# Weighted combine of expert outputs on one core: who copies the weights of a round, and how the first tail tokens are loaded

## The chip, the cores and the metric

The kernel runs on one NeuronCore of one Trainium2 chip. The metric is the device time of one execution in microseconds; the number compared is the median over several executions. One execution is also profiled, and the profile's times are counted from the start of its span.

## The reference

For each of 16 x 1024 = 16384 tokens there are 8 expert outputs of 512 numbers and 8 weights. The result is the weighted sum over the experts.

```python
batch, seq, n_experts, expert_dim = 16, 1024, 8, 512
weights = combine_weights[..., np.newaxis]
return np.sum(expert_outputs * weights, axis=2).astype(np.float32)
```

All is float32. The input is 268.4 MB, the output 33.6 MB.

## The kernel before, in words

**Tiles.** Every partition owns 121 tokens that are worked in a loop of 11 rounds (`ROUNDS`) of 11 tokens (`R`), and 7 tail tokens (`TAIL`). `ring` holds one round's input, 11 tokens of 8 x 512 numbers in each partition. A round is cut into three chunks, of 4, 4 and 3 tokens (`CHUNKS`, line 41); a chunk of 4 tokens is 8.39 MB over the 128 partitions, and a round with its store is 25.95 MB. There is one ring, so a chunk of the next round can be loaded only when the same chunk of this round has been worked. `sums` holds one round's results, also once.

**SyncE** (`loads_and_last_stores`, lines 126 to 145) issues all input loads in order, on one DMA queue: per round three chunk loads, then the tail tokens, then the last round's store, then the two stores of the tail. Before each chunk load it waits for two semaphores:

```python
sync.wait_ge(copied, (n - 1) * C + c + 1)
sync.wait_ge(w_set, n * C + c + 1)
```

**GpSimd** (`weights_and_store`, lines 160 to 171) copies a chunk's weights of the coming round from `w_t`, where all weights lie, to `w_c`, where the loop of VectorE reads them at a fixed address; it does so when `copied` says that the chunk of this round is worked and copied out. `w_set` counts these copies. At one place, after the first copy for the last round, it also runs `store_apart` (lines 106 to 117): a part of the store of round 9, in three DMAs of its own, and a fourth small DMA (`turn`, line 119). These are counted on `rest_out`, and ScalarE waits for them before the first copy of round 10 (line 190).

**VectorE** (`terms`, lines 229 to 295) does the sums: per chunk one product over the chunk (line 250), then for experts 1 to 7 one multiply-and-add for each token (line 242), in place in `ring`. In chunks of 4 tokens two tokens take turns, in the chunk of 3 all three. The last multiply-and-add of each token counts `done` up by 1 (line 235).

**ScalarE** (`copies_stores_and_diagonals`, lines 173 to 203) waits for a chunk's `done`, copies the results to `sums` (line 175), counts `copied`, and after the third chunk issues the round's store on its own DMA queue (line 185). It begins the copies of a round only when the store of the round before has landed (`stored`, line 179), as there is one `sums`.

**The tail.** The 7 tail tokens go to the ring places of chunks 0 and 1: one load for tokens 0 to 2, then four loads of one token (`tail_loads`, line 65). TensorE forms the first 3 to 5 terms of each tail token with diagonal matrices that ScalarE makes (lines 205 to 227); VectorE adds the rest (lines 269 to 295). TensorE starts when the first tail load has landed (line 217).

Of the kernel before, what the change touches and what calls it, by code (L numbers as in the profile page):

```python
# [10 lines left out]
def kernel(  # L11
# [21 lines left out]
    nc = tc.nc  # L33
# [6 lines left out]
    R = 11  # L40
    CHUNKS = [(0, 4), (4, 4), (8, 3)]
    C = len(CHUNKS)
    T_P = T // P
    ROUNDS = T_P // R
    LOOP = ROUNDS * R
    TAIL = T_P - LOOP
# [3 lines left out]
    SHARED = ROUNDS - 2  # L50
# [8 lines left out]
    x_t = x[cut:T].rearrange("(p j) e d -> p j e d", j=TAIL)  # L59
# [2 lines left out]


    pe_e = [4, 4, 3, 4, 4, 5, 4]
    tail_loads = [(0, 3)] + [(j, 1) for j in range(3, TAIL)]
    tail_stores = [(0, 5), (5, 2)]
    loads = [k for k, (j, m) in enumerate(tail_loads) for _ in range(m)]
    diags = [(j, e) for j in range(TAIL) for e in range(pe_e[j])]

    one = ctx.enter_context(tc.tile_pool(name="one", bufs=1))  # L70
# [1 line left out]
    ring = one.tile([P, R, E, D], fp32, name="ring")  # L72
    sums = one.tile([P, R, D], fp32, name="sums")
    w_t = one.tile([P, T_P, E], fp32, name="w_t")
    w_c = one.tile([P, R, E], fp32, name="w_c")
# [3 lines left out]
    diag = one.tile([P, DIAGS, P], fp32, name="diag")  # L79
    ps = psum.tile([P, TAIL, D], fp32, name="ps")  # L80

    last_sums = ring[:, TAIL + 1, 1 : 1 + TAIL]

    sem = tc.alloc_semaphore
    w_in = sem("w_in")
    w_set = sem("w_set")
    loaded = [sem(f"loaded{c}") for c in range(C)]
    copied = sem("copied")
    here = sem("here")
    stored = sem("stored")  # L90
    rest_out = sem("rest_out")
    step = sem("step")
    done = sem("done")
    tail_in = [sem(f"tail_in{k}") for k in range(len(tail_loads))]
    tail_out = nc.alloc_semaphore("tail_out")
    id_set = sem("id_set")
    diag_set = sem("diag_set")
# [6 lines left out]
        queue.dma_start(out=o_r[n, :, first:], in_=flat[:, first:]).then_inc(stored, 16)  # L104

    def store_apart(gpsimd):
        flat = sums.rearrange("p g d -> p (g d)")
        gpsimd.wait_ge(copied, SHARED * C + 1)
        gpsimd.dma_start(  # L109
            out=o_r[SHARED, 0:OURS, 0 : APART * D], in_=flat[0:OURS, 0 : APART * D]  # L110
        ).then_inc(rest_out, 16)
        for k in range(2):
            part = slice(k * APART * D // 2, (k + 1) * APART * D // 2)
            gpsimd.dma_start(out=o_r[SHARED, OURS:P, part], in_=flat[OURS:P, part]).then_inc(  # L114
                rest_out, 16
            )
        turn(gpsimd, 13, 4)

    def turn(gpsimd, k, b):

        gpsimd.dma_start(  # L121
            out=spare[0:k, b : b + 4].rearrange("p (i j) -> p i j", i=2)[:, :, 0:1],
            in_=w[0 : 2 * k].rearrange("(p i) e -> p i e", i=2)[:, :, 0:1],
        ).then_inc(rest_out, 16)

    def loads_and_last_stores(sync):
        for n in range(ROUNDS):
            for c, (r, m) in enumerate(CHUNKS):
                if n:
                    sync.wait_ge(copied, (n - 1) * C + c + 1)  # L130
                    sync.wait_ge(w_set, n * C + c + 1)
                part = slice(r, r + m)
                sync.dma_start(out=ring[:, part], in_=x_r[n, :, part]).then_inc(loaded[c], 16)
                if n == 0 and c == 0:
                    sync.dma_start(out=w_t[:, 0:LOOP], in_=w_r).then_inc(w_in, 16)
                    sync.dma_start(out=w_t[:, LOOP:T_P], in_=w_x).then_inc(w_in, 16)
        for k, (j, m) in enumerate(tail_loads):
            sync.wait_ge(copied, (ROUNDS - 1) * C + (j + m - 1) // 4 + 1)
            sync.dma_start(out=ring[:, j : j + m], in_=x_t[:, j : j + m]).then_inc(tail_in[k], 16)
        store(sync, ROUNDS - 1)  # L140
        for j, m in tail_stores:
            sync.wait_ge(done, LOOP - SHARED * R + j + m)
            sync.dma_start(out=o_t[:, j : j + m], in_=last_sums[:, j : j + m]).then_inc(
                tail_out, 16
            )

    def identity(gpsimd):
# [8 lines left out]
            pattern=[[-1, P]],  # L156
            channel_multiplier=1,
        ).wait_op(id_set, 2, "sem-ge").then_inc(id_set, 1)

    def weights_and_store(gpsimd):  # L160
        turn(gpsimd, 4, 0)
        gpsimd.wait_ge(w_in, 32).then_inc(stored, 16)
        for n in range(ROUNDS):
            for c, (r, m) in enumerate(CHUNKS):
                if n:
                    gpsimd.wait_ge(copied, (n - 1) * C + c + 1)
                gpsimd.tensor_copy(  # L167
                    out=w_c[:, r : r + m], in_=w_t[:, n * R + r : n * R + r + m]
                ).then_inc(w_set, 1)
                if n == SHARED + 1 and c == 0:  # L170
                    store_apart(gpsimd)

    def copies_stores_and_diagonals(scalar):
        def copy(r, m):
# [38 lines left out]

    def first_terms(tensor):
        for k, (j, e) in enumerate(diags):
            if k == 0:
                tensor.wait_ge(tail_in[0], 16)
            if e == 0:
                tensor.wait_ge(tail_in[loads[max(j, 2)]], 16)
            tensor.wait_ge(diag_set, k + 1)  # L220
            tensor.matmul(  # L221
                ps[:, j],
                lhsT=diag[:, k % DIAGS],
                rhs=ring[:, j, e],
                start=e == 0,
                stop=e == pe_e[j] - 1,
            ).then_inc(product, 1)

    def terms(vector):
        last = {}  # L230

        def count(i, g, e):

            if e == E - 1:
                i.then_inc(done, 1)
            else:
                i.then_inc(step, 1)
                last["all"] = last.get("all", 0) + 1
                last[g] = last["all"]

        def fused(total, g, e, weight, before):
            return vector.scalar_tensor_tensor(  # L242
                out=total, in0=ring[:, g, e], scalar=weight, in1=before, op0=mult, op1=add
            )

        vector.wait_ge(w_set, C)
        with nc.Fori(0, ROUNDS, engines=OrderedEngineSet([vector.engine])):  # L247
            for c, (r, m) in enumerate(CHUNKS):
                take(vector, loaded[c], 16)
                i = vector.tensor_tensor(  # L250
                    out=ring[:, r : r + m, 0],
                    in0=ring[:, r : r + m, 0],
                    in1=w_c[:, r : r + m, 0:1].to_broadcast([P, m, D]),
                    op=mult,
                )
                i.then_inc(step, 1)
                last["all"] = last.get("all", 0) + 1
                last.update((g, last["all"]) for g in range(r, r + m))
                for some in [(r, r + 1), (r + 2, r + 3)] if m == 4 else [range(r, r + m)]:
                    for e in range(1, E):  # L260
                        for k in some:
                            i = fused(ring[:, k, 0], k, e, w_c[:, k, e : e + 1], ring[:, k, 0])
                            i.wait_op(step, last[k], "sem-ge")
                            count(i, k, e)
            take(vector, step, last["all"])

        last.clear()

        def tail_term(j, e, end):
            total, x, weight = last_sums[:, j], ring[:, j, e], w_t[:, LOOP + j, e : e + 1]  # L270
            if e > pe_e[j]:
                i = fused(total, j, e, weight, total)
                i.wait_op(step, last[j], "sem-ge")
            elif j < TAIL - 1:
                i = fused(total, j, e, weight, ps[:, j])
                i.wait_op(product, sum(pe_e[: j + 1]), "sem-ge")
            else:
                i = vector.tensor_scalar_mul(out=total, in0=x, scalar1=weight)  # L278
                i.wait_op(tail_in[-1], 16, "sem-ge")
            count(i, j, end)  # L280

        j = TAIL - 1
        for k in range(j - 1):
            for e in range(pe_e[k], E):
                tail_term(k, e, e)

        vector.wait_ge(copied, ROUNDS * C)
        for e in range(pe_e[j], E):
            tail_term(j, e, -1)
            if e + 1 < E:  # L290
                tail_term(j - 1, e + 1, e + 1)
        vector.wait_ge(step, last[j])  # L292
        i = vector.tensor_tensor(out=last_sums[:, j], in0=last_sums[:, j], in1=ps[:, j], op=add)  # L293
        i.wait_op(product, len(diags), "sem-ge")
        count(i, j, E - 1)

    with tc.tile_critical(no_gpsimd_drain=True):  # L297
        loads_and_last_stores(nc.sync)
        identity(nc.gpsimd)
        weights_and_store(nc.gpsimd)  # L300
        copies_stores_and_diagonals(nc.scalar)
        first_terms(nc.tensor)
        terms(nc.vector)
# [35 lines left out]
```

## Time and profile before

| what | value |
|---|---|
| median of 3 runs | 757.14 us (756.41 to 757.99) |
| the profiled execution: its time, its span | 756.85 us, 755.2 us |
| busy share of the span: VectorE, GpSimd, ScalarE, TensorE | 86%, 10%, 9%, 4% |
| moved by DMA, mean rate | 302.54 MB, 401 GB/s |
| busy share of the DMA engines by queue: SyncE's, ScalarE's, GpSimd's | 85.2%, 8.7%, 0.2% |
| granted TensorE clock, mean | 0.999 |

The time of an execution is 1.65 us more than its span. The DMA share of a stretch is the mean over 16 DMA engines of the time that their packets took; a packet is put down whole where it is recorded, so over a few us the share can pass 1, and it is read over longer stretches. The busy time of an engine does not count its waits. Idle time of an engine is put down to what released it.

### The profile page before, as it was taken

The numbers are of one execution on the slowest core, as the hardware profiler recorded it, in microseconds if no ns is written. First come the engines' busy times: TensorE is split into PE (matmuls) and PEld (weight loads), VectorE is DVE, ScalarE is ACT, GpSimd is POOL, SyncE is SP. The second block draws the span as 40 slices with busy tenths as digits, with TensorE's granted clock in tenths as the row PEclk, the third lists the DMA queues.
The fourth block names the chain that finished last, engine by engine and source line by source line (L and its number), as shares of the span: only waits on it lengthen the run. The fifth ranks groups of instructions, "written<-read, shape, count | busy, mean of one in ns | idle before, by whom it ended". The sixth has DMA issues, their size and how long they took to land. (4 is left out here: it accounts for less than half of the span.)

```text
span 755.2 us, 1471 instructions
## 1 busy us (share of the span) xinstructions
PE 27.3 (4%) x56; PEld 11.6 (2%) x56; DVE 652.2 (86%) x909; ACT 68.8 (9%) x63; POOL 74.6 (10%) x45
## 2 busy tenths in 40 slices
PE   0000000000000000000000000000000000000067
PEld 0000000000000000000000000000000000000023
DVE  0699999497999949799994899999479999948998
ACT  0011002001101100110110001011010101101132
POOL 0000006000000600000140000033000005300000
PEclk9999999999999999999999999999999999999999
DMA  9999994999999699999959999996999997899998
GB/s 389 423 437 445 415 427 200 413 403 448 444 439 408 250 382 437 444 444 427 430 240 391 429 444 444 410 410 278 410 432 422 444 434 330 350 385 432 456 408 373
DMA packets 7907, 302.54 MB, mean 401 GB/s; under 512 B 1112, under 2 KB 1112, under 8 KB 1504
## 3 DMA queue, kind: packets, MB, share of 16 engines
q1 hardware_dynamic: 6192, 273.68, 85.2%
q10 hardware_dynamic: 1440, 28.31, 8.7%
q0 software_dynamic: 272, 0.52, 0.2%
q14 instruction: 3, 0.02, 0.0%
HBM read 268.96 MB, written 33.55 MB: 401 GB/s over the span
## 5 line engine op out<-in xcount | busy, mean ns | idle before, releaser
L242 DVE SCALAR_TENSOR_TENSOR ring<-ring,w_c 128x512 f32<-128x512 f32 x847 | 564.1, 745 | 1.2
L250 DVE TENSOR_TENSOR ring<-ring,w_c 128x2048 f32<-128x2048 f32 (+1 forms) x33 | 69.6, 2108 | 98.1 <-DVEq L212 98.1
L167 POOL COPY w_c<-w_t 128x32 f32<-128x32 f32 (+1 forms) x33 | 71.0, 2154 | 585.3 <-ACTq L183 522.0
L175 ACT COPY sums<-ring 128x2048 f32<-128x2048 f32 (+1 forms) x33 | 57.9, 1756 | 669.9 <-ACTq L212 580.6
L221 PE MATMUL ps<-ring,diag 128*128 128x512 f32 x56 | 27.3, 652 | 723.4 <-DMA ring<-in_expert_outputs_dram 723.4
L221 PEld LDWEIGHTS ps<-ring,diag 128*128 128x128 f32 x56 | 11.6, 210 | 738.2 <-DMA ring<-in_expert_outputs_dram 723.4
L242 DVE SCALAR_TENSOR_TENSOR ring<-ring,w_t 128x512 f32<-128x512 f32 x21 | 15.4, 750 | 0.6
L207 ACT ACTIVATE diag<-ident,w_t 128x128 f32<-128x128 f32 x28 | 9.6, 393 | 4.6 <-PE ps L221 4.6
L242 DVE SCALAR_TENSOR_TENSOR ring<-ring,w_t,ps 128x512 f32<-128x512 f32 x6 | 4.5, 742 | 0.0
L121 POOL DMA_DIRECT2D spare<-in_combine_weights_dram x2 | 1.4, 694 | 0.3 <-issue 0.3
L177 ACT ACT_TABLE_LOAD x1 | 1.3, 1283 | 0.9 <-SPq L297 0.9
L114 POOL DMA_DIRECT2D out_dram<-sums x2 | 1.0, 518 | 0.0
L293 DVE TENSOR_TENSOR ring<-ring,ps 128x512 f32<-128x512 f32 x1 | 0.7, 687 | 0.1
L109 POOL DMA_DIRECT2D out_dram<-sums x1 | 0.6, 572 | 0.0
L278 DVE TENSOR_SCALAR ring<-ring,w_t 128x512 f32<-128x512 f32 x1 | 0.5, 480 | 0.0
L150 POOL TENSOR_SCALAR_AFFINE_SELECT ident<-ident 128x128 f32<-128x128 f32 x1 | 0.3, 287 | 0.1
L149 POOL MEMSET ident<- 128x128 f32 x1 | 0.2, 204 | 0.0
L177 ACT COPY warm<-warm 128x1 f32<-128x1 f32 x1 | 0.2, 191 | 0.0
L148 POOL MEMSET warm<- 128x2 f32 x1 | 0.1, 99 | 0.5 <-SPq L297 0.5
L323 POOL MEMSET const-float32-0.0<- 128x1 f32 x1 | 0.1, 100 | 0.2 <-issue 0.2
L323 POOL MEMSET const-uint8-127<- 128x1 uint8 x1 | 0.1, 103 | 0.0
L323 POOL MEMSET const-bfloat16-1.0<- 128x1 bf16 x1 | 0.1, 102 | 0.0
(1 smaller groups left out, 0.1 us busy)
## 6 DMA issues: line engine op xcount, KB each, us to landing
ring<-in_expert_outputs_dram SPq DMA_DIRECT2D x12, 6144.0 KB, 41.4
out_dram<-sums ACTq DMA_DIRECT2D x9, 2816.0 KB, 28.1
ring<-in_expert_outputs_dram SPq DMA_DIRECT2D x4, 2048.0 KB, 22.5
out_dram<-sums SPq DMA_DIRECT2D x1, 2816.0 KB, 17.0
out_dram<-sums ACTq DMA_DIRECT2D x1, 2304.0 KB, 30.3
out_dram<-ring SPq DMA_DIRECT2D x1, 1280.0 KB, 5.6
out_dram<-ring SPq DMA_DIRECT2D x1, 512.0 KB, 3.0
w_t<-in_combine_weights_dram SPq DMA_DIRECT2D x1, 484.0 KB, 22.5
```

Source lines behind the costliest of these rows:

```text
L109: gpsimd.dma_start(out=o_r[SHARED, 0:OURS, 0 : APART * D], in_=flat[0:OURS, 0 : APART * D]).then_inc(rest_out, 16)
L114: gpsimd.dma_start(out=o_r[SHARED, OURS:P, part], in_=flat[OURS:P, part]).then_inc(rest_out, 16)
L121: gpsimd.dma_start(out=spare[0:k, b : b + 4].rearrange("p (i j) -> p i j", i=2)[:, :, 0:1], in_=w[0 : 2 * k].rearrange("(p i) e -> p i e", ...
L167: gpsimd.tensor_copy(out=w_c[:, r : r + m], in_=w_t[:, n * R + r : n * R + r + m]).then_inc(w_set, 1)
L175: return scalar.copy(out=sums[:, r : r + m], in_=ring[:, r : r + m, 0])
L177: scalar.copy(out=warm[:, 1:2], in_=warm[:, 0:1]).wait_op(id_set, 1, "sem-ge")
L207: return scalar.mul(out=diag[:, k % DIAGS], in_=ident, mul=w_t[:, LOOP + j, e : e + 1]).then_inc(diag_set, 1)
L221: tensor.matmul(ps[:, j], lhsT=diag[:, k % DIAGS], rhs=ring[:, j, e], start=e == 0, stop=e == pe_e[j] - 1,).then_inc(product, 1)
L242: return vector.scalar_tensor_tensor(out=total, in0=ring[:, g, e], scalar=weight, in1=before, op0=mult, op1=add)
L250: i = vector.tensor_tensor(out=ring[:, r : r + m, 0], in0=ring[:, r : r + m, 0], in1=w_c[:, r : r + m, 0:1].to_broadcast([P, m, D]), op=mult,)
L278: i = vector.tensor_scalar_mul(out=total, in0=x, scalar1=weight)
L293: i = vector.tensor_tensor(out=last_sums[:, j], in0=last_sums[:, j], in1=ps[:, j], op=add)
```

## The change

VectorE waits once for all weights to have landed. At the head of each round of its loop it copies the round's 11 x 8 weights to `w_c` itself, and the first product of each chunk waits for `step` 1, which that copy counts. GpSimd copies no weights; of its work only `store_apart` is left, behind the wait for the weights (moved there with the first `turn`). SyncE no longer waits for `w_set` before a load. In VectorE's loop all multiply-and-adds count `step`, and behind each chunk VectorE waits for the last of them and then counts `done` up by the number of tokens. The seven tail tokens are loaded by seven loads of one token, and TensorE waits for the load of the token that it begins.

```diff
     pe_e = [4, 4, 3, 4, 4, 5, 4]
-    tail_loads = [(0, 3)] + [(j, 1) for j in range(3, TAIL)]
     tail_stores = [(0, 5), (5, 2)]
-    loads = [k for k, (j, m) in enumerate(tail_loads) for _ in range(m)]
...
+    w_l = w_t[:, 0:LOOP].rearrange("p (n g) e -> p n g e", g=R)
...
-    w_set = sem("w_set")
...
-    tail_in = [sem(f"tail_in{k}") for k in range(len(tail_loads))]
+    tail_in = [sem(f"tail_in{j}") for j in range(TAIL)]
...
     def store_apart(gpsimd):
+        turn(gpsimd, 4, 0)
+        gpsimd.wait_ge(w_in, 32).then_inc(stored, 16)
         flat = sums.rearrange("p g d -> p (g d)")
         gpsimd.wait_ge(copied, SHARED * C + 1)
...
                 if n:
                     sync.wait_ge(copied, (n - 1) * C + c + 1)
-                    sync.wait_ge(w_set, n * C + c + 1)
...
-        for k, (j, m) in enumerate(tail_loads):
-            sync.wait_ge(copied, (ROUNDS - 1) * C + (j + m - 1) // 4 + 1)
-            sync.dma_start(out=ring[:, j : j + m], in_=x_t[:, j : j + m]).then_inc(tail_in[k], 16)
+        for j in range(TAIL):
+            sync.wait_ge(copied, (ROUNDS - 1) * C + j // 4 + 1)
+            sync.dma_start(out=ring[:, j : j + 1], in_=x_t[:, j : j + 1]).then_inc(tail_in[j], 16)
...
-    def weights_and_store(gpsimd):
-        turn(gpsimd, 4, 0)
-        gpsimd.wait_ge(w_in, 32).then_inc(stored, 16)
-        for n in range(ROUNDS):
-            for c, (r, m) in enumerate(CHUNKS):
-                if n:
-                    gpsimd.wait_ge(copied, (n - 1) * C + c + 1)
-                gpsimd.tensor_copy(
-                    out=w_c[:, r : r + m], in_=w_t[:, n * R + r : n * R + r + m]
-                ).then_inc(w_set, 1)
-                if n == SHARED + 1 and c == 0:
-                    store_apart(gpsimd)
...
         for k, (j, e) in enumerate(diags):
-            if k == 0:
-                tensor.wait_ge(tail_in[0], 16)
             if e == 0:
-                tensor.wait_ge(tail_in[loads[max(j, 2)]], 16)
+                tensor.wait_ge(tail_in[j], 16)
...
-        vector.wait_ge(w_set, C)
-        with nc.Fori(0, ROUNDS, engines=OrderedEngineSet([vector.engine])):
+        vector.wait_ge(w_in, 32)
+        with nc.Fori(0, ROUNDS, engines=OrderedEngineSet([vector.engine])) as n:
+            i = vector.tensor_copy(out=w_c, in_=w_l[:, n])
+            i.then_inc(step, 1)
+            last["all"] = 1
             for c, (r, m) in enumerate(CHUNKS):
                 take(vector, loaded[c], 16)
...
-                i.then_inc(step, 1)
+                i.wait_op(step, 1, "sem-ge").then_inc(step, 1)
...
-                            count(i, k, e)
+                            count(i, k, -1)
+                vector.wait_ge(step, last["all"]).then_inc(done, m)
             take(vector, step, last["all"])
...
-        weights_and_store(nc.gpsimd)
+        store_apart(nc.gpsimd)
```

## Rows read from the trace of the kernel before

**Rows 1.** The page's second part: the DMA's busy tenths in 40 slices, and its total.

```profile
DMA  9999994999999699999959999996999997899998
...
DMA packets 7907, 302.54 MB, mean 401 GB/s; under 512 B 1112, under 2 KB 1112, under 8 KB 1504
```

**Rows 2.** Window between two dips: stretch, its length, busy time of each engine, PEclk, DMA share, GB/s.

```profile
126.90:248.50 121.60, 0.00 (x0) 0.00 (x0) 106.49 (x150) 8.64 (x5) 6.47 (x6) 1.00 1.00 427
```

**Rows 3.** Windows of 15 us around the dips, and the first and last 5 us.

```profile
115.00:130.00 15.00, 0.00 (x0) 0.00 (x0) 14.96 (x22) 2.11 (x2) 11.66 (x2) 1.00 0.34 129
245.00:260.00 15.00, 0.00 (x0) 0.00 (x0) 14.96 (x22) 1.90 (x1) 12.01 (x2) 1.00 0.45 175
...
635.00:650.00 15.00, 0.00 (x0) 0.00 (x0) 14.96 (x22) 1.90 (x1) 13.04 (x6) 1.00 0.55 217
0.00:5.00 5.00, 0.00 (x0) 0.00 (x0) 0.00 (x0) 1.47 (x2) 1.47 (x8) 1.00 0.63 210
750.00:755.20 5.20, 0.71 (x2) 0.00 (x0) 2.06 (x4) 0.00 (x0) 0.00 (x0) 0.83 0.56 230
```

**Rows 4.** Timeline around the first dip: start, us, engine, line, operation [idle before].

```profile
113.31 1.90 ACT L175 COPY sums<-ring 128x2048 f32<-128x2048 f32 x1 [28.63 <-ACTq L212]
115.32 11.26 POOL L167 COPY w_c<-w_t 128x32 f32<-128x32 f32 x1 [29.96 <-ACTq L183]
124.76 1.75 DVE L250 TENSOR_TENSOR ring<-ring,w_c 128x1536 f32<-128x1536 f32 x1
...
126.66 1.11 SPq L133 DMA_DIRECT2D ring<-in_expert_outputs_dram  x2
```

**Rows 5.** All weight copies of GpSimd: duration in ns, least, median, greatest.

```profile
L167 POOL COPY w_c<-w_t x33: 197/400/12922, 24.8 to 660.8; 128x32 f32<-128x32 f32 x22, 128x24 f32<-128x24 f32 x11
```

**Rows 6.** Waits of SyncE's queue: us in total, times, longest.

```profile
SPq L131 <- POOL w_c L167: 646.3, 30, 45.5
```

**Rows 7.** DMA issues: us to landing; loads issued at 126.7 and 176.4, all looped stores.

```profile
ring<-in_expert_outputs_dram SPq DMA_DIRECT2D x1, 24.6
...
ring<-in_expert_outputs_dram SPq DMA_DIRECT2D x1, 33.8
...
DMA to landing us min/median/max: 26.6/28.1/31.5
```

**Rows 8.** VectorE: its first chunk, the next round's start, small operations and gaps.

```profile
25.54 2.29 DVE L250 TENSOR_TENSOR ring<-ring,w_c 128x2048 f32<-128x2048 f32 x1 [25.54 <-DVEq L212]
27.87 18.64 DVE L242 SCALAR_TENSOR_TENSOR ring<-ring,w_c 128x512 f32<-128x512 f32 x28
...
83.01 2.28 DVE L250 TENSOR_TENSOR ring<-ring,w_c 128x2048 f32<-128x2048 f32 x1
...
L242 DVE SCALAR_TENSOR_TENSOR ring<-ring,w_c 128x512 f32<-128x512 f32 x847 | 564.1, 745 | 1.2
...
L278 DVE TENSOR_SCALAR ring<-ring,w_t 128x512 f32<-128x512 f32 x1 | 0.5, 480 | 0.0
...
729.37 0.32 issue
...
746.27 0.63 issue
```

**Rows 9.** GpSimd's own DMAs: first issue, next copy, the last one's time to landing.

```profile
645.21 0.57 POOL L109 DMA_DIRECT2D out_dram<-sums  x1
...
647.45 0.59 POOL L167 COPY w_c<-w_t 128x32 f32<-128x32 f32 x1
...
spare<-in_combine_weights_dram POOLq DMA_DIRECT2D x1, 0.1 KB, 42.8
```

**Rows 10.** Timeline of the tail: TensorE's matmuls, VectorE's first and last operation.

```profile
723.42 27.29 PE L221 MATMUL ps<-ring,diag 128*128 128x512 f32 x56 [723.42 <-DMA ring<-in_expert_outputs_dram]
...
731.01 0.74 DVE L242 SCALAR_TENSOR_TENSOR ring<-ring,w_t,ps 128x512 f32<-128x512 f32 x1
...
751.48 0.69 DVE L293 TENSOR_TENSOR ring<-ring,ps 128x512 f32<-128x512 f32 x1
```

## Prediction

> **What bounds the kernel now.** I read the page's slices first. VectorE has the largest busy share, yet the slices of the DMA are the ones to read: they are full nearly everywhere, with five dips about 130 us apart [rows 1]. Between the first two dips the window gives a DMA share of 1.00 at 427 GB/s [rows 2]. So the kernel is bound by transfers, except in the dips. The windows around these give the lost time: shares of 0.34, 0.45 and 0.55 in the first, second and fifth, and the third (375 to 390) and fourth (505 to 520) read 0.45 like the second [rows 3]. Idle DMA time there is 15 x (0.66 + 3 x 0.55 + 0.45) = 41.4 us. The start loses 5 x 0.37 = 1.9 us and the end 5.2 x 0.44 = 2.3 us [rows 3].
>
> Then the timeline at the first dip. ScalarE's copy of chunk 0 ends at 115.2; GpSimd's weight copy starts at 115.32 and takes 11.26 us; SyncE issues the next load 0.08 us after it ends [rows 4]. The median of these copies is 0.40 us, the greatest 12.9 [rows 5]. Five are long, from this one to that, all for chunk 0 and one in each dip. VectorE streams multiply-and-adds through all of it, and the copy comes free just after the product of the next chunk (124.76 + 1.75 = 126.51, against 126.58). SyncE's waits confirm that GpSimd ends 30 of its waits [rows 6].
>
> The Trainium skill (SBUF — State Buffer, § Who interferes with whom) has the rule for it: a VectorE instruction with two SBUF inputs contends with a GpSimd instruction that reads SBUF. The row agrees that the copy is shut out, but not with its size: the page lets the other side block for one instruction, which here would be 2.3 us at most, and the hold was 11.26.
>
> **The change part by part.**
>
> *The copies leave GpSimd.* A load now waits for `copied` alone. In the dips that moves the issue from 126.66 to about 115.3, while the queue still works: it ran dry at about 117. All 41.4 us of idle time fall if nothing else is late there. Next in line is the store: ScalarE's copy of chunk 0 at 113.31 had itself waited for the store of the round before [rows 4], which lands 26.6 to 31.5 us after its issue [rows 7]. Is that early enough? A load issued into a dry queue lands after 24.6 us; the one at 176.4, which waited for its store in the same way but had a short weight copy, landed after 33.8 us [rows 7]. It stood 9.2 us behind other loads, so the queue had that much left. This is the margin of the store gate where GpSimd doesn't hold, and I take it for all rounds: no new idle time. The ordinary short copies lay in that margin too, and are worth nothing.
>
> *VectorE's loop gets longer.* A round takes 83.01 - 25.54 = 57.5 us without waits [rows 8]. Added per round: (a) One copy of 88 numbers. No row has it on VectorE; between GpSimd's 0.20 us for 32 [rows 5] and VectorE's 0.48 for 512 [rows 8] I take 0.3. (b) Three waits at the chunk ends. Without a wait the next instruction starts about 0.08 us before the last one ends (28 multiply-and-adds of 0.745 us fill 18.64 us, where end to end they would take 20.9); with one, 27.87 - 27.83 = 0.04 us after [rows 8]. With the semaphore's own instruction I take 0.16 each, 0.5 in all; the upper bound is the 0.63 us gap in front of a waiting VectorE instruction [rows 8], 1.9 in all. Less than nothing is excluded, as a wait takes no work away. (c) The jump of the loop now lies behind a finished chunk: 0.32 us of issue was seen there [rows 8], I take 0.5 with its neighbours. (d) The first product waits for the copy: 0.04. Together 1.3 us, at most 0.5 + 1.9 + 0.5 + 0.1 = 3.0, so a round takes 58.8 us, at most 60.5. The DMA needs 25.95 MB / 427 GB/s = 60.8 us a round. The additions hide in VectorE's waits for loads, with 2.0 us a round to spare, at the bound 0.3. Behind each chunk wait stand only the next chunk's instructions; ScalarE, which waits for `done`, gets it 0.1 us later and has the margin of 9.2.
>
> *The start.* VectorE began at 25.54, after GpSimd's copies; its own copy moves that by some 0.3 us either way. The loads already queued don't see it: nothing.
>
> *GpSimd's own DMAs* come after `copied` 28 as before, without a long copy ahead: some 12 us earlier in the round. Four issues took 647.45 - 645.21 = 2.2 us and the last landed 42.8 us later [rows 9], 45 in all, while ScalarE needs them a round later, after 60.8. Nothing, with 15.8 us to spare.
>
> *The tail.* Two more loads cost SyncE two issues while the queue is full: nothing. TensorE can start two tokens earlier, 2 x 2.10 MB / 427 GB/s = 9.8 us. Its chain (723.42 + 27.29 = 750.7) and VectorE's (751.48 + 0.69 = 752.2) ended together [rows 10], but the DMA is full until 750 and idles for 2.3 us in all behind that [rows 3]. So the early start is worth between nothing and 2.3 us; I take nothing.
>
> **The sum.** 755.2 - 41.4 = 713.8 us of span. Cross-check by bytes: 302.54 MB / 427 GB/s = 708.5, with start and end 712.7. VectorE alone would end sooner: 25.5 + 11 x 58.8 + 24.2 (its tail's first operation, 731.0 [rows 10], to the span's end) = 696.5. The profiled time is 1.65 us above its span: 715.5 us. The sum is made against the profiled execution (756.85), 0.3 us under the median.
>
> The Trainium skill (DMA: Bandwidth & Descriptors, § Specifications) puts the fabric's ceiling at 435 GB/s. At that rate the same bytes would give an estimate of 695.5 us and a time of 701. The window stops at 427, and the measurement decides.
>
> **The rivals.**
>
> *The store takes GpSimd's place.* With the queue always full, stores share the engines with loads in all rounds; if they land at 43 us in place of 31.5 at most, the margin of 9.2 is passed by 2.3 us in some nine rounds: 715.5 + 21 = 736. For it: ScalarE's copy already waits on it. Against: the 28 us were measured in stretches with a full queue. Chance 0.08.
>
> *VectorE becomes the bound.* Its round would have to take over 60.8. At 62, 25.5 + 682 + 24.2 + 1.65 = 733. It needs additions of 4.5 us, above my bound of 3.0. Chance 0.04.
>
> *The change doesn't do what it says: the long spans are only recorded long.* GpSimd's spans are rough. If the port held the copy for one instruction at most (the mechanism of one VectorE instruction of 2.3 us), the load was held by something else that stays, and the gain is at most what shows as short copies, which the margin hides: about 757. Against: SyncE's issue 0.08 us behind the copy's end, five times. The Trainium skill's rule named above would have it so. Chance 0.03.
>
> *Slower: GpSimd's DMAs are held as its copies were.* They are now issued in the middle of chunk 1 of round 9, where the five copies were held; before, they came early in chunk 2, where nothing was. One held by 12.9 us fits in the 15.8. It decides when the four holds together pass this, and from about 70 us on the kernel is slower than before, as ScalarE's first copy of the last round, and with it all tail loads, stand behind it. If one passes in each round: 12.9 + 3 x 60.8 = 195, 195 + 45 - 60.8 = 179 us late, less 9 of queued loads: 715.5 + 170 = 886. Against: one passage in chunk 2 let all four through. Chance 0.03.
>
> The same section of the Trainium skill says that the contention is with a GpSimd instruction that reads SBUF, not with one that only writes; by that, writing descriptors would not be held. No run here shows it yet.
>
> **How the numbers follow.** The forecast has 0.82, with 711 to 721 as its own range: down 2.3 us by the tail and some by the rate, up by 0.5 us a round of idle DMA. Faster by over 0.2%, about what this measurement can tell: 0.82 + 0.08 + 0.04 = 0.94. Same 0.03, slower 0.03. The predicted time is 715.5. The range of 710 to 727 holds the forecast and the milder part of the first two rivals.
>
> **What would show it.** DMA slices with no dips, a share near 1.00 from 5 to about 708 us; the load for chunk 0 issued 0.1 us behind ScalarE's copy; VectorE's waits spread over most rounds at 1 to 4 us, no longer 4 and 10 in every second; chunk spacing in VectorE 20.9 to 21.1. It would be wrong if dips stay (and then: who released SyncE), if VectorE never waits, or if ScalarE's first copy of round 10 waits for `rest_out`.

## The result, and the profile after

The changed kernel takes 707.22 us (median of 6 runs, 706.25 to 707.64) against 756.76 (6 runs in the same comparison): a ratio of 0.9343, with a 95% interval of 0.9331 to 0.9355. The forecast was 715.5 with a range of 710 to 727. The direction and the mechanism were right, but the time lies 2.8 us below the range: the gain was 49.5 us in place of 41, and one term of the sum was too small.

The profiled execution has a span of 705.9 us. The page of the changed kernel, its first three parts:

```profile
PE 28.0 (4%) x56; PEld 11.8 (2%) x56; DVE 656.8 (93%) x920; ACT 68.9 (10%) x63; POOL 3.7 (1%) x12
...
DMA  9999999999999999999999999999999999999997
...
q1 hardware_dynamic: 6480, 273.68, 89.9%
q10 hardware_dynamic: 1440, 28.31, 9.3%
```

The five dips of [rows 1] are gone. The shares of the three queues add up to 94.1% of the span before and 99.4% now, so the DMA engines' idle time falls from 755.2 x (1 - 0.941) = 44.6 us to 705.9 x (1 - 0.994) = 4.2: 40.4 us of the gain is idle time, close to the forecast 41.4. The rest is in the line of q1, SyncE's queue. It moves the same 273.68 MB, and its packets took 85.2% of 755.2 = 643.4 us before and 89.9% of 705.9 = 634.6 us now: 8.8 us less per DMA engine, for the same bytes. 40.4 + 8.8 = 49.2 of the 49.3 us between the two spans.

The same split is seen in one window, 110 us long, that lies between two dips of the kernel before. First the kernel before, then the changed one (columns as in [rows 2]):

```profile
132.00:242.00 110.00, 0.00 (x0) 0.00 (x0) 94.89 (x132) 6.92 (x5) 1.38 (x4) 1.00 0.99 425
```

```profile
132.00:242.00 110.00, 0.00 (x0) 0.00 (x0) 107.56 (x152) 8.64 (x5) 0.00 (x0) 1.00 1.00 434
```

The share is as good as full in both, and the rate is 425 and 434 GB/s. Such a rate is good to a few GB/s only, as whole packets are counted at the window's ends; but in the windows of the same length between the later dips (from 262, 392 and 522) it is 425 to 431 before and 434 to 437 now. A full share doesn't say that the engines move as much as they can; one has to read the GB/s beside it.

VectorE's waits and its first rounds in the changed kernel (the waits view, then the timeline):

```profile
ACT sums L161 <- ACTq L198: 566.2, 29, 43.7
...
DVE ring L237 <- DVEq L198: 10.7, 22, 1.6
DVE w_c L232 <- DVEq L198: 7.1, 10, 0.8
```

```profile
24.74 0.21 DVE L232 COPY w_c<-w_t 128x88 f32 x1 [24.74 <-DMA w_t<-in_combine_weights_dram]
84.00 0.21 DVE L232 COPY w_c<-w_t 128x88 f32 x1 [0.77 <-DVEq L198]
143.21 0.21 DVE L232 COPY w_c<-w_t 128x88 f32 x1 [0.71 <-DVEq L198]
```

The 98 us of load waits of the kernel before have shrunk to 10.7 in 22 entries, of which the new chunk waits, 0.26 us each, make up more than half. A round takes 143.21 - 84.00 = 59.2 us, 1.7 more than the 57.5 of [rows 8]. With 25.95 MB / 434 GB/s = 59.8 us a round, transfers and VectorE now run almost in step.

### The profile page after: what moved, and what is told of

Its sections match the earlier page's. It is cut to its first block, busy times and chain, and to the rows that moved or that the text cites. A ratio compares the mean times of both kernels' runs of the same rounds, so it can differ in the third digit from the quotient of the medians.

```text
span 705.9 us, 1465 instructions
## 1 busy us (share of the span) xinstructions
PE 28.0 (4%) x56; PEld 11.8 (2%) x56; DVE 656.8 (93%) x920; ACT 68.9 (10%) x63; POOL 3.7 (1%) x12
## 3 DMA queue, kind: packets, MB, share of 16 engines
q1 hardware_dynamic: 6480, 273.68, 89.9%
## 5 line engine op out<-in xcount | busy, mean ns | idle before, releaser
L237 DVE TENSOR_TENSOR ring<-ring,w_c 128x2048 f32<-128x2048 f32 (+1 forms) x33 | 69.8, 2114 | 11.1 <-DVEq L198 10.7
L232 DVE COPY w_c<-w_t 128x88 f32 x11 | 2.3, 206 | 31.8 <-DMA w_t<-in_combine_weights_dram 24.7
```

The lines of the kernel that those rows point to most:

```text
L232: i = vector.tensor_copy(out=w_c, in_=w_l[:, n])
L237: i = vector.tensor_tensor(out=ring[:, r : r + m, 0], in0=ring[:, r : r + m, 0], in1=w_c[:, r : r + m, 0:1].to_broadcast([P, m, D]), op=mult,)
```

## The experiments

### The loads don't wait for GpSimd; VectorE does

```diff
 kernel before
-                    sync.wait_ge(w_set, n * C + c + 1)
...
-        vector.wait_ge(w_set, C)
...
+                take(vector, w_set, 1)
                 take(vector, loaded[c], 16)
```

> The kernel before, with one edit: GpSimd still copies all weights, but loads no longer wait for the copies; VectorE waits for a chunk's copy in front of the chunk's product. If the hold of the loads was the whole cost (theory), the long copies of 11 to 13 us stay in GpSimd's rows, the dips are gone, and the time is 705 to 712 us. If GpSimd's copies cost something beside the hold, for example longer load packets (rival), the dips are gone but the SyncE queue's packets still take 643 us in all, as in the kernel before, not 635 as in the changed one, and the time is 713 to 720.

Measured: 705.51 us, ratio 0.9326 (0.9311 to 0.9340). GpSimd's timeline and the q1 line of the page:

```profile
115.01 11.07 POOL L166 COPY w_c<-w_t 128x32 f32<-128x32 f32 x1 [30.15 <-ACTq L182]
...
171.80 14.76 POOL L166 COPY w_c<-w_t 128x32 f32<-128x32 f32 x1 [29.49 <-ACTq L182]
```

```profile
q1 hardware_dynamic: 6192, 273.68, 90.1%
```

All weights are still copied by GpSimd, and its copies for chunk 0 are held in nearly every round now, nine times, for 11 to 15 us. It costs nothing, since only VectorE waits for them, a round later. So what the change removed was one wait of SyncE. The packets of q1 took 90.1% of 703.9 = 634.2 us, as in the changed kernel: GpSimd's copies don't lengthen them.

### Dips put in by another hand

```diff
 changed kernel
-                    sync.wait_ge(copied, (n - 1) * C + c + 1)
+                    sync.wait_ge(copied, (n - 1) * C + c + 1 + (c == 0 and n % 2 == 0))
```

In every second round the load of chunk 0 now waits until chunk 1, too, is copied out.

> The changed kernel, with dips put in by another hand: in rounds 2, 4, 6, 8 and 10 the load of chunk 0 waits until chunk 1 of the round before is copied out, some 15 us later than needed. No GpSimd copy is in it. Each dip should idle the DMA for 11 to 14 us, 55 to 70 in all. If a dip itself makes the packets behind it longer (theory), the SyncE queue's packets take about 643 us in place of 635 and the time is 770 to 785. If the longer packets of the kernel before came from GpSimd's copies (rival), they stay at 635 and the time is the idle time alone above 707, 760 to 775.

Measured: 767.66 us, ratio to the kernel before 1.0143 (1.0128 to 1.0159). The page, and the window of above:

```profile
DMA  9999994999999599999959999986999997799997
...
q1 hardware_dynamic: 6480, 273.68, 84.0%
q10 hardware_dynamic: 1440, 28.31, 8.6%
```

```profile
132.00:242.00 110.00, 0.00 (x0) 0.00 (x0) 94.19 (x133) 6.74 (x4) 0.00 (x0) 1.00 1.00 426
```

The time of 767.66 lies in the rival's span and 2 us under the theory's, so the time doesn't decide; it is low because the dips were shorter than I expected: idle time is 766.3 x (1 - 0.928) = 55.2 us, 51 above the changed kernel. The packets decide: q1 took 84.0% of 766.3 = 643.7 us, what the theory asked for, and the rate between two dips is down to 426. 51.0 us of idle time and 9.1 us of longer packets make up 60.1 of the 60.4 us above the changed kernel. With no GpSimd copy in this kernel, the longer packets come with the dips: 9 us for five, some 1.8 us each on average.

### ScalarE copies the weights

```diff
 kernel before
-                    sync.wait_ge(w_set, n * C + c + 1)
...
-                gpsimd.tensor_copy(
...
+                scalar.copy(out=w_c[:, r : r + m], in_=w_n[:, n, r : r + m]).then_inc(here, 1)
                 copy(r, m).then_inc(here, 1)
-                scalar.wait_ge(here, c + 1).then_inc(copied, 1)
+                scalar.wait_ge(here, 2 * c + 2).then_inc(copied, 1)
```

> The kernel before, with the weight copies made by ScalarE in front of its copy of the same chunk's results; GpSimd copies none, no load waits for GpSimd, and VectorE has no copy and no chunk waits. Tail loads as before. If the hold of the loads was all (theory), the dips are gone, VectorE's round without load waits is 57.5 us again, and the transfers alone set the time: 704 to 707. If the changed kernel owes part of its gain to VectorE's own copying (rival), 709 to 716.

Measured: 705.89 us, ratio 0.9334 (0.9319 to 0.9348). VectorE's round is 82.68 - 25.21 = 57.5 us again, and it waits 47.6 us for loads in all. The time is within 1.5 us of the changed kernel's, and within 0.2 us of the 705.69 us that VectorE's own copy takes with the same tail loads (two experiments below). Who copies the weights doesn't matter, so long as no load waits for it behind VectorE's stream.

### One chunk wait in place of three

```diff
 changed kernel
-                            count(i, k, -1)
-                vector.wait_ge(step, last["all"]).then_inc(done, m)
+                            count(i, k, e if c < C - 1 else -1)
+                if c == C - 1:
+                    vector.wait_ge(step, last["all"]).then_inc(done, m)
```

> The changed kernel, where chunks 0 and 1 count done from their last terms again; only the last chunk of a round keeps the wait on VectorE. The wait looks like 0.34 us of VectorE's time in the changed kernel's rows (0.26 idle, where instructions used to overlap by 0.08). So a round without load waits should take 59.2 - 2 x 0.34 = 58.5 us. If the transfers set the time (theory), it stays at 706 to 707.5; if VectorE's round does (rival), it falls by up to 11 x 0.68 = 7.5 us, to 700.

Measured: 707.27 us, ratio 0.9353 (0.9340 to 0.9366). VectorE's timeline:

```profile
83.62 0.21 DVE L232 COPY w_c<-w_t 128x88 f32 x1 [0.78 <-DVEq L198]
...
142.13 0.21 DVE L232 COPY w_c<-w_t 128x88 f32 x1 [0.71 <-DVEq L198]
```

A round without load waits takes 142.13 - 83.62 = 58.5 us, as worked out from 0.34 us a wait, and the time doesn't move. The transfers set it, not VectorE.

### The tail: three tokens in one load, or apart

The two edits are the tail's part of the diff, undone in the changed kernel and done alone in the kernel before.

> The changed kernel, with the first three tail tokens in one load again. If the loads of their own gain nothing (theory, as predicted), the same as the changed kernel within 1 us, 706 to 708. If they brought the part of the gain that was not predicted (rival), 711 to 715.

> The kernel before, with the first three tail tokens in loads of their own and nothing else. Theory: TensorE starts some 9 us earlier, the end is then set by the last transfers, and the gain is 0 to 2.3 us: 754.5 to 757. Rival: the tail gain is several us, 749 to 753.

Measured: 705.69 us for the first (ratio 0.9325, 0.9312 to 0.9338), 758.87 for the second, slower than the kernel before: 1.0029 (1.0018 to 1.0041). I had both wrong: loads of their own cost time. As 705.69 and 707.22 come from two separate comparisons, both kernels were run once more together:

> The changed kernel once more, on the same chip as its version with three tail tokens in one load, to settle a difference of 1.5 us between them: 706.5 to 707.6.

> The changed kernel with the first three tail tokens in one load, once more, beside the changed kernel itself on the same chip. If loads of their own cost 1.5 us by letting TensorE run out of diagonals (theory), 705 to 706.2; if the difference was that between chips (rival), the same as the changed kernel within 0.5 us.

Measured: 706.61 us (706.41 to 708.05) and 705.85 us (705.50 to 706.10), ratios 0.9348 and 0.9332; the runs don't overlap, but the intervals of the ratios do. So in the changed kernel the cost is 0.8 to 1.5 us, at the edge of what is told apart, and in the kernel before a clear 2.2. The two kernels' timelines, in which each product of TensorE with a diagonal stands as two matmuls: first the changed kernel, then the one with three in one load:

```profile
666.57 8.50 PE L205 MATMUL ps<-ring,diag 128*128 128x512 f32 x16 [666.57 <-ACT diag L193]
680.29 1.47 ACT L161 COPY sums<-ring 128x1536 f32<-128x1536 f32 x1 [11.81 <-DVEq L252]
...
681.66 2.44 ACT L193 ACTIVATE diag<-ident,w_t 128x128 f32<-128x128 f32 x8
...
682.20 19.52 PE L205 MATMUL ps<-ring,diag 128*128 128x512 f32 x40 [7.13 <-ACT diag L193]
...
702.49 0.69 DVE L281 TENSOR_TENSOR ring<-ring,ps 128x512 f32<-128x512 f32 x1
```

```profile
673.43 26.15 PE L207 MATMUL ps<-ring,diag 128*128 128x512 f32 x56 [673.43 <-DMA ring<-in_expert_outputs_dram]
...
701.00 0.69 DVE L283 TENSOR_TENSOR ring<-ring,ps 128x512 f32<-128x512 f32 x1
```

With loads of their own TensorE starts 6.9 us earlier, and uses up the 8 diagonals that ScalarE has made. ScalarE stands in its wait for the loop's last chunk, so TensorE idles 7.13 us until 682.2. Windows of the changed kernel, and one of the other (PEclk, the granted clock, is the third number from the end):

```profile
675.00:681.00 6.00, 0.08 (x1) 0.00 (x0) 5.58 (x9) 0.71 (x1) 0.00 (x0) 0.89 1.00 426
681.00:684.00 3.00, 1.80 (x2) 0.84 (x3) 2.89 (x5) 3.00 (x9) 0.00 (x0) 0.50 1.01 429
684.00:687.00 3.00, 3.00 (x6) 1.23 (x5) 2.63 (x4) 0.91 (x3) 0.00 (x0) 0.59 0.99 421
687.00:690.00 3.00, 3.00 (x9) 1.33 (x8) 2.72 (x4) 1.46 (x4) 0.00 (x0) 1.00 1.02 433
```

```profile
675.00:678.00 3.00, 3.00 (x6) 1.20 (x5) 3.00 (x5) 0.00 (x0) 0.00 (x0) 1.00 1.03 437
```

While TensorE stood still, the granted clock fell to 0.50, which is 1.2 of 2.4 GHz, and from 684 to 687, at 0.59, six matmuls took the 3 us that nine take from 687 on at 1.00. With three in one load TensorE starts late, but never stops, and its chain ends at 673.43 + 26.15 = 699.6, against 682.20 + 19.52 = 701.7. It too has six matmuls in 3 us behind its start, where the row puts the clock at 1.00; so the slow beginning isn't special to the pause, and the pause makes TensorE go through it twice. The difference adds up: 7.1 us of pause and 8.50 + 19.52 - 26.15 = 1.9 us of slower matmuls, less the 6.9 us of the earlier start, are the 2.1 us by which the chain ends later.

### More diagonals ahead

```diff
 changed kernel, ScalarE, ahead of its wait for the last chunk
+    AHEAD = 15
...
                     for k in range(DIAGS):
                         diagonal(scalar, k)
+                    for k in range(DIAGS, AHEAD):
+                        diagonal(scalar, k).wait_op(product, k - DIAGS + 1, "sem-ge")
```

> The changed kernel, where ScalarE makes 15 diagonals, not 8, before it waits for the last chunk of the loop. In the changed kernel TensorE used up the 8 by 675, idled 7 us until ScalarE came free, and then worked at a granted clock of 0.50 for some us. Theory: with 15 it does not idle so long, its chain ends earlier, and the cost of the three loads of their own (1.5 to 2.3 us) is gone or turned to a gain: 704.5 to 706. Rival: the end is set by the last transfers and stays at 706.5 to 707.5.

Measured: 705.67 us, ratio 0.9334 (0.9321 to 0.9347). The windows again:

```profile
681.00:684.00 3.00, 1.80 (x5) 0.60 (x4) 2.89 (x5) 2.81 (x9) 0.00 (x0) 1.00 1.01 431
684.00:687.00 3.00, 2.85 (x7) 0.95 (x5) 2.89 (x5) 1.32 (x4) 0.00 (x0) 1.00 1.03 437
```

The granted clock stays at 1.00 from 675 to 687, TensorE's pauses are 0.3 to 1.2 us, each ended by a load, and VectorE waits for it 0.4 us in all, against 1.2 in the changed kernel. This is the expected 704.5 to 706: the loss goes, and no more, since the transfers end there too.

All together (ScalarE's copies, single loads, 15 diagonals ahead):

> Candidate for the best: ScalarE copies the weights, no chunk waits on VectorE, the first three tail tokens in loads of their own, and 15 diagonals ahead. If the transfers alone set the end (theory), it is 704 to 706, no better than each part alone. If the parts add (rival), 702.5 to 704.

Measured: 705.56 us, ratio 0.9328 (0.9315 to 0.9341). Five versions lie between 705.5 and 705.9; the parts don't add. All are clearly faster than the kernel before; against the changed kernel's 706.61 and 707.22 they gain 0.7 to 1.7 us, at the edge of what is told apart. The least edit among them is the first experiment's.

### What holds GpSimd's copy

> The kernel before, where in chunks of 4 tokens all four take turns in VectorE's stream, not two and two. GpSimd's copies and the loads' wait for them stay. In the kernel before a copy in the chunk of 3 tokens, whose tokens all take turns, got through at the end of the running instruction (0.4 to 0.6 us), and in the middle of a chunk with pairs it was held to the end of the next chunk's product. If the pairs are what holds it (theory), the copies all take under 1 us and the time is 704 to 710. If a copy is held in the middle of chunk 1 whatever the turn (rival), five copies of 11 to 13 us and 755 to 758 stay.

Measured: 756.29 us, ratio 0.9999 (0.9990 to 1.0008), with the five long copies as before. That the pairs hold it is refuted.

> The kernel before, with the chunks in the order 4, 3, 4 tokens: the copy for chunk 0 is now asked for while VectorE works the chunk of 3. If that chunk's stream lets a copy through wherever it is asked for, as it did early in it (theory), all copies take under 1 us and the time is 703 to 710. If it is the place in the stream, early or middle, that decides (rival), the copies for chunk 0 are held to the end of the next chunk's product, for some 8 to 13 us, and the time is 740 to 760.

Measured: 718.25 us (two runs, 716.54 and 719.96), ratio 0.9496 (0.9470 to 0.9521). Neither figure was met. GpSimd's and VectorE's timeline:

```profile
105.22 14.00 DVE L242 SCALAR_TENSOR_TENSOR ring<-ring,w_c 128x512 f32<-128x512 f32 x21
```

```profile
115.51 3.78 POOL L167 COPY w_c<-w_t 128x32 f32<-128x32 f32 x1 [30.54 <-ACTq L183]
120.92 1.10 POOL L167 COPY w_c<-w_t 128x24 f32<-128x24 f32 x1 [1.63 <-ACTq L183]
```

The copies for chunk 0 were held for 3 to 5.4 us: this one from 115.51 to 119.29, 0.07 us after the stream of the 3-token chunk ended (105.22 + 14.00), where VectorE then waited for a load. So the hold is no matter of 3 or 4 tokens: a copy asked for in the middle of a stream got in where the stream stopped, and as what was left of the stream is shorter here, so is the hold. Copies asked for in the first 2.2 us of a chunk got in at the end of the running instruction, in at most 1.1 us. Why early and middle differ is open.

This run also says something of the price of a late load. Its line of q1:

```profile
q1 hardware_dynamic: 6192, 273.68, 89.7%
```

Its span of 715.0 us is 11.1 above the 703.9 of the first experiment. Only about 3.6 us of that is idle time (6.4 against 2.8); q1's packets took 89.7% of 715.0 = 641.4 us, 7.2 more. So packets get longer also where the queue is only just about to run dry, and 1.8 us is no fixed price of a dip. The order of the chunks differs here as well, so this run alone doesn't single out the cause.

## Why the prediction was right, and where it was wrong

**What bounds the kernel: right.** Transfers, except for five dips made by one GpSimd copy each, held behind VectorE's stream. The first experiment shows that the load's wait alone was the cost.

**The copies leave GpSimd: right in its idle time (40.4 us, forecast 41.4), wrong in the price of a dip.** This is the step that failed. I priced a dip at the time in which nothing moves, 15 x (1 - share). But packets behind a dip take longer, by some 1.8 us a dip, which the share counts as busy time. Five dips cost 40.4 us of idle time and 8.8 us of longer packets, where the sum had 41.4 and nothing. The dips put in by hand show it (643.7 us for the packets of q1), and the kernels without dips, whoever copies, have 634 to 635.

**The cross-check by bytes failed for the same reason.** It took 427 GB/s from a window that begins right behind a dip [rows 2], so both ways to the sum stood on a disturbed stretch, and agreed. From 150 to 242, which leaves out its first 23 us and its last 6, the rate is 434. The trace of before had an undisturbed one, ahead of the first dip:

```profile
5.00:115.00 110.00, 0.00 (x0) 0.00 (x0) 89.28 (x124) 6.95 (x4) 1.67 (x6) 1.00 1.01 433
```

At 433 GB/s the bytes take 698.7 us; with 4.2 of start and end and 1.65 around the span that is 704.5, and every version without a tail loss measures 705.5 to 705.9. That it comes so close is partly luck: the window from 10 to 110 gives 430, which is 5 us more. "The window stops at 427, and the measurement decides" was wrong as the floor: the estimate of 701 from the Trainium skill's 435 GB/s (DMA: Bandwidth & Descriptors, § Specifications) was 6 us off, my own 8. The range had little room below: 2.3 us for the tail and some 3 for the rate.

**The store's margin: the size off, the conclusion right.** I read 9.2 us, as the difference between two landing times. In the changed kernel loads for chunk 0 behind a store land 24.4 to 28.9 us after their issue, against 24.6 from a dry queue, which by that measure leaves as little as nothing. But the measure was wrong. The load issued at 115.0 had one ahead of it that landed at 120.0, and over all rounds the load ahead lands 5.0 to 8.4 us after the issue; at the 176.4 of [rows 7] it landed 14.4 us after. So the measure reads some 5 us too little, and the margin shrank from 14.4 to 5.0 at the least. The stores still land after 27.1 to 28.0 us, and no dip shows. What a longer store would do was not tried.

**VectorE's loop: 1.7 us a round, where I took 1.3 and at most 3.0.** The copy takes 0.21 (taken 0.3), a chunk wait 0.34 (taken 0.16); two of these and the loop's head, which holds the third and the copy and takes about 1.0, give the 1.7. That it hides was right, with 59.8 - 59.2 = 0.6 us a round to spare in place of 2.0: with two of the waits gone the time is the same.

**The tail: wrong in sign.** "Worth between nothing and 2.3 us" left out what TensorE needs beside the tokens, the diagonals, and the engine that makes them. The cost is 0.8 to 2.2 us.

**The rivals.** GpSimd's own DMAs were not held, although they were issued in the middle of VectorE's chunk 1:

```profile
591.11 0.57 POOL L109 DMA_DIRECT2D out_dram<-sums x1 [588.54 <-ACT sums L161]
...
592.69 0.64 POOL L121 DMA_DIRECT2D spare<-in_combine_weights_dram  x1
```

The first takes the same 0.57 us as in [rows 9], 0.3 us behind the copy of results that it waits for (588.90 + 1.90 = 590.80), in the middle of VectorE's stream of 585.2 to 603.8. This agrees with the Trainium skill (SBUF — State Buffer, § Who interferes with whom), that a VectorE instruction with two SBUF inputs contends with a GpSimd instruction that reads SBUF, and not with one that only writes it. The same section's hold of one instruction fits copies asked for early in a stream, and not the ones in the middle, with 11 to 15 us. The long spans were real, as the rival with no gain is refuted by the time. Neither the stores (28.0 us at most) nor VectorE's loop became the bound.

## What to carry to other kernels

A wait between two engines that is short on most rounds can be long on a few; look at the greatest duration of a small operation, not its mean, and at who waits for it. Take a rate for a forecast from a stretch with no disturbance in it or shortly before it, from more than one window, and read GB/s beside the share. An operation started earlier gains only if all that feeds it comes earlier too.

## What the runs showed of the hardware that was not expected

A dip of the DMA queue costs more than its length. 64 KB load packets take 2.42 us in the median in all kernels; in the packet records of the kernel before, 221 of 2816 took over 2.52 us, mostly in groups of about 16, two groups behind each dip (at the restart, and some 18 us later where the round's store starts), against 38 in the changed kernel, all in the first three rounds. Over the median they add up to 11.1 us per DMA engine before and 1.8 in the changed kernel: the 9.3 between them agrees with the 8.8 us of q1. The dips put in by hand bring back 200 such packets. Why a restart does this wasn't tried.

A GpSimd copy of 32 numbers per partition that is asked for in the middle of a stream of VectorE's multiply-and-adds is held for the rest of the stream, and for the next chunk's product where VectorE doesn't pause, up to 14.8 us in all, and not for one instruction. What it needs to get in is open.
